# A two-layer diffusion trunk on one core: the first layer's gates and ups by seven half-block products instead of eight

## The chip, the core and the metric

The kernel runs on one core of a Trainium2 chip. The core has five engines with instruction streams of their own: TensorE (PE, matrix products; PEld is its weight load), VectorE (DVE), ScalarE (ACT), GpSimd (POOL) and SyncE (SP), which here issues all DMA transfers between DRAM and on-chip memory. Matrix products collect in PSUM, everything else stands in SBUF. The metric is the device time of one execution in microseconds. The kernel before takes 2279.43 us (median of 3 runs, 2278.52 to 2282.81).

## The reference

A trunk of two layers over 512 latent and 256 context tokens of width 1024, all in 32-bit floats. Each layer has an adaptive norm, one input projection for three mixers (RWKV-7, latent attention, mLSTM), one output projection, a second adaptive norm and a SwiGLU feed-forward network of hidden width 2816. What matters here is the second half of a layer:

```python
xl = xl + gt1_l * (concatenate([ya_l, yb_l, ym_l]) @ w_out[i])
xl = xl + gt2_l * swiglu(modulate(rmsnorm(xl, norm2_g[i]), sh2_l, sc2_l), ffn_w_in[i], ffn_w_out[i])
if ctx_out:                      # layer 0 alone: the context tokens too, with their own modulation
    ...
def swiglu(h, w_in, w_out):
    gate, up = jnp.split(h @ w_in, 2, axis=-1)
    return (jax.nn.silu(gate) * up) @ w_out
```

The modulation's vectors (`sh`, `sc`, `gt`, six of width 1024 for each layer) are products of `silu(c)` and `silu(c_ctx)` with a 1024 x 6144 matrix per layer. So layer 0's feed-forward network works on 768 tokens, layer 1's on 512.

## The kernel before

Everything is kept transposed: 128 features on the partitions, tokens along the free dimension. A 32-bit product is made of three products in a rounded format: each operand is split into `hi` (a rounded copy, by ScalarE) and `lo` (the rest, by VectorE; helper `split`, L227 and L228), and `gemm` (L262) adds hi·hi, hi·lo and lo·hi of each 128-row block of K in PSUM. `weight` (L235) loads a block of weights through a ring of two buffers and splits it.

The part that the change touches is the end of each layer, in one scope of the layer loop:

- **Output projection** (`add` with which = 0). `silu_rows` first spreads `silu(c)` over the partitions (transposes L311, copies L312), for the modulation's products on VectorE. Then for each of eight 128-row blocks m of the output: load and split the weights, 24 x 512 and 24 x 256 columns of matmul, residual sum on VectorE (L1323), squares and sums for the next norm (L337, L338; on POOL for the first four m). The last four m are worked span by span (first the 512 latent tokens, then the 256 context tokens), so that the norm of the first span is finished while the second is computed. `norm_page` multiplies X by the scale (L364, into one of three `hu` buffers), modulates it (L365) and splits it into the pages `hpage` (even pages on VectorE, odd ones on POOL).
- **Feed-forward network in three parts** of 8, 7 and 7 hidden tiles (PARTS). For a hidden tile j the gate's and the up's weights are loaded and split, and for each token span 24 + 24 matmuls run. tanh (L1490), two VectorE operations (L1491, L1492) and a split give the hidden tile as `hid`, of which eight stay in SBUF. After each part `add` with which = 1 multiplies the part's hidden tiles with the output weights for all eight m and adds them to X.
- **Modulation.** `mod_dve` loads 128 x 1024 weights (L318) and makes two VectorE products with row sums (L320), one for context and one for latent tokens. They fill VectorE's free time: four products (two blocks) after each hidden tile of layer 0, two after each m of the first two output parts, and what is left of them in the third.

All loops are written out at build time. A scheduler simulates the engines and sets the order of instructions on each of them; `issue_after` holds an instruction back until a given one was placed. SP's queue of DMA issues is in order too. PSUM has five buffers for these products (`gm`).

## Time and profile before

| What | us |
| --- | --- |
| Median of the runs (3) | 2279.43 |
| Profiled execution, its own time | 2283.55 |
| Its span, first to last instruction | 2281.8 |
| TensorE busy | 2159.2 (95%) |
| VectorE busy | 1381.9 (61%) |
| ScalarE busy | 844.7 (37%) |
| GpSimd busy | 314.2 (14%) |

Outside the span lie 1.75 us of the profiled execution. It was 4.1 us longer than the median of the runs, so a difference worked out in the trace is taken from 2283.55 and then brought to the median. Busy time alone does not say what a stage is worth. The stage of the change is layer 0's feed-forward network, from 747 to 1307 us of the span, and the rows further down are mostly read from there.

### The profile page before, as it was taken

The numbers are of one execution on the slowest core, as the hardware profiler recorded it, in microseconds if no ns is written. First come the engines' busy times: TensorE is split into PE (matmuls) and PEld (weight loads), VectorE is DVE, ScalarE is ACT, GpSimd is POOL, SyncE is SP. The second block draws the span as 40 slices with busy tenths as digits, with TensorE's granted clock in tenths as the row PEclk, the third lists the DMA queues.
The fourth block names the chain that finished last, engine by engine and source line by source line (L and its number), as shares of the span: only waits on it lengthen the run. The fifth ranks groups of instructions, "written<-read, shape, count | busy, mean of one in ns | idle before, by whom it ended". The sixth has DMA issues, their size and how long they took to land.

```text
span 2281.8 us, 36365 instructions
## 1 busy us (share of the span) xinstructions
PE 2159.2 (95%) x14604; PEld 1780.9 (78%) x14604; DVE 1381.9 (61%) x2706; ACT 844.7 (37%) x1527; POOL 314.2 (14%) x482
## 2 busy tenths in 40 slices
PE   7999997997999999999999999999898998999999
PEld 4788886784668788888888878787685677888887
DVE  6687777895547766554444455788796545334343
ACT  4433333664552421122122354433473544222231
POOL 1022322332201100000000111113142211000000
PEclk9999997897999999999999989999697998999999
DMA  7241112232115334344432312211232122323323
GB/s 289 84 153 52 62 41 74 77 88 56 42 70 155 100 114 146 111 129 135 133 112 83 109 52 63 73 57 39 85 100 59 35 74 83 101 94 94 100 92 102
DMA packets 87352, 211.99 MB, mean 93 GB/s; under 512 B 10248, under 2 KB 33680, under 8 KB 86544
## 3 DMA queue, kind: packets, MB, share of 16 engines
q1 hardware_dynamic: 87184, 209.67, 29.2%
q8 instruction: 115, 1.88, 0.3%
q14 instruction: 53, 0.43, 0.1%
HBM read 187.62 MB, written 22.02 MB: 92 GB/s over the span
## 4 chain that ended last, share of the span: by engine, by line
PE 81%; DVE 10%; ACT 4%; DMA 2%; issue 2%; POOL 1%; SPq 0%; DVEq 0%; ACTq 0%; POOLq 0%
PE gm L262 57%; PE po L1034 4%; PE psm L585 2%; PE inv L660 2%; PE st L1028 1%; DVE cT L320 1%; PE st L1029 1%; PE st L1030 1%; PE mx L1008 1%; PE psm L514 1%; PE pB L700 1%; DVE wl L228 1%; PE psm L573 1%; ACT hu L365 1%; PE up L246 1%
## 5 line engine op out<-in xcount | busy, mean ns | idle before, releaser
L262 PE MATMUL gm<-hpage,wh 128*128 128x512 f32 (+1 forms) x3744 | 1001.7, 355 | 15.3 <-ACT hpage L227 8.9
L262 PEld LDWEIGHTS gm<-hpage,wh 128*128 128x128 f32 x3744 | 664.2, 191 | 119.8 <-ACT hpage L227 11.0
L262 PE MATMUL gm<-hpage,wl 128*128 128x512 f32 (+1 forms) x1872 | 657.4, 353 | 1.9 <-DVE wl L228 1.8
L227 ACT ACTIVATE wh<-wr 128x1024 fp32r<-128x1024 f32 (+2 forms) x214 | 221.6, 1036 | 560.7 <-PE gm L262 457.6
L262 PEld LDWEIGHTS gm<-hpage,wl 128*128 128x128 f32 x1872 | 358.1, 191 | 50.6 <-DVE wl L228 2.5
L228 DVE TENSOR_TENSOR wl<-wr,wh 128x1024 fp32r<-128x1024 f32 (+2 forms) x214 | 258.2, 1207 | 186.9 <-ACT wh L227 185.1
L262 PE MATMUL gm<-hid,wh 128*128 128x512 f32 (+1 forms) x1056 | 282.6, 356 | 0.0
L262 PEld LDWEIGHTS gm<-hid,wh 128*128 128x128 f32 x1056 | 185.6, 188 | 32.2
L262 PE MATMUL gm<-hid,wl 128*128 128x512 f32 (+1 forms) x528 | 187.4, 356 | 0.0
L1323 DVE SCALAR_TENSOR_TENSOR X<-gm,mod,X 128x512 f32<-128x512 f32 (+1 forms) x100 | 64.0, 643 | 191.0 <-PE gm L262 187.7
L320 DVE CUSTOM_DVE_ANT_0 cT<-wd,cB,mod_b 128x1024 f32<-128x1024 f32 x140 | 177.7, 1300 | 1.1 <-DMA wd<-in_mod_d 0.7
L1492 DVE SCALAR_TENSOR_TENSOR ft<-ft,gm 128x512 f32<-128x512 f32 x66 | 39.5, 598 | 153.0 <-PE gm L262 152.7
L1010 DVE TENSOR_REDUCE mr<-mx 128x1 fp32r<-128x768 f32 (+1 forms) x80 | 67.9, 848 | 83.8 <-PE mx L1008 83.6
L1034 PE MATMUL po<-pe,hpage 128*128 128x512 f32 (+1 forms) x224 | 112.2, 590 | 0.5 <-ACT pe L1032 0.4
L262 PEld LDWEIGHTS gm<-hid,wl 128*128 128x128 f32 x528 | 99.0, 188 | 16.1
L338 POOL TENSOR_TENSOR acc<-acc,sq 128x512 f32<-128x512 f32 (+1 forms) x15 | 23.9, 1601 | 604.0 <-ACT sq L337 604.0
L1032 ACT ACTIVATE pe<-st 128x512 f32<-128x512 f32 (+1 forms) x112 | 62.9, 563 | 89.8 <-PE st L1030 88.7
L227 ACT ACTIVATE hid<-ft 128x512 fp32r<-128x512 f32 x66 | 36.2, 549 | 128.4 <-DVE ft L1492 128.4
L1028 PE MATMUL st<-k,k 97*128 97x512 f32 (+1 forms) x112 | 78.0, 698 | 4.7 <-ACT k L1015 4.1
L1490 ACT ACTIVATE ft<-gm 128x512 f32<-128x512 f32 x66 | 33.9, 514 | 90.4 <-PE gm L262 90.3
L1008 PE MATMUL mx<-k,k 96*128 96x256 f32 (+1 forms) x144 | 46.3, 396 | 17.1 <-DVE mr L1010 9.9
L585 PE MATMUL psm<-pr,kb 64*128 64x128 f32 (+1 forms) x384 | 57.7, 308 | 1.4 <-POOL pr L555 1.4
(425 smaller groups left out, 3128.5 us busy)
## 6 DMA issues: line engine op xcount, KB each, us to landing
wr<-in_ffn_in SPq DMA_DIRECT2D x88, 512.0 KB, 3.5
wd<-in_mod_d SPq DMA_DIRECT2D x86, 512.0 KB, 3.8
wr<-in_w_in SPq DMA_DIRECT2D x44, 512.0 KB, 3.6
wr<-in_ffn_out SPq DMA_DIRECT2D x34, 448.0 KB, 3.4
wr<-in_w_out SPq DMA_DIRECT2D x20, 512.0 KB, 3.7
wr<-in_ffn_out SPq DMA_DIRECT2D x16, 512.0 KB, 3.6
zs<-ze SPq DMA_DIRECT2D x26, 256.0 KB, 2.0
X<-in_xT SPq DMA_DIRECT2D x16, 384.0 KB, 6.4
```

The costliest lines, as they stand in the source:

```text
L227: ac.activation(hi, src, AF.Copy)
L228: return en.tensor_tensor(lo, src, hi.bitcast(F32), ALU.subtract)
L262: pe.matmul(ps, x[:, j], act[k][y][:, a:b], start=(i == 0 and n == 0), stop=(i == len(kl) - 1 and n == 2))
L320: ve.tensor_tensor_reduce(out=t[:, s], in0=w, in1=cb[:, s], scale=1.0, scalar=modb[:, l, m:m + 1], op0=ALU.mult, op1=ALU.add, accum_out=mo ...
L585: pe.matmul(pa[j][:, p, c], flat(kb[hr, d, p, c]), flat(pr[hr, d, p, c, 0:nq]), start=True, stop=True)
L660: i = pe.matmul(v8(o)[hr, q], a[hr, d, p, c], b[hr, d, p, c], start=True, stop=True)
L1008: pe.matmul(ps[:, a - k0:b - k0], qh[0:96, n * P:(n + 1) * P], kh[0:96, a:b], start=True, stop=True)
L1010: ve.tensor_reduce(mr[:, n - q0:n - q0 + 1], ps[:, :T - k0], AX.X, ALU.max)
L1028: pe.matmul(ps, kh[0:97, ks], qh[0:97, qs], start=True, stop=False)
L1032: ac.activation(e, ps, AF.Exp, scale=QK_SCALE)
L1034: pe.matmul(po[:, :w], v, e, start=(kt == kts[0]), stop=(kt == kts[-1]))
L1323: return ve.scalar_tensor_tensor(X[:, m, a:b], ps, mods[l][:, 24 * which + 16 + m, s:s + 1], X[:, m, a:b], ALU.mult, ALU.add)
```

## The change

In layer 0 the second half is written anew (`ffn`, with `residuals`, `halves`, `resplit`, `gate_up`, `swiglu`, `fetch` and `mods_on`); layer 1 keeps the old loops. Two hidden tiles are computed as before (PLAIN = 2). For the other 20, the gate's and the up's weights of one tile are read as one matrix of 2 x 2 blocks (gate and up by two halves of K, 128 x 512 each), the normed tokens as another (two halves of K by two halves of 384 tokens), and Winograd's form of Strassen's product is used: seven products of half blocks in place of eight, with sums of blocks before and after.

- The token sums are made once (`halves`): eight subtractions on VectorE, eight on POOL, and twelve splits on VectorE and ScalarE. For this the normed pages are kept unsplit in `ru`.
- The weight sums are made for each tile: four on POOL, of 128 x 512. Five half blocks of weights are split beside the gate's whole block.
- Each product is 4 K blocks x 3 matmuls of 384 columns. Out of PSUM come one copy on ScalarE and seven sums on VectorE; then two tanh, two VectorE operations of 384 columns and one of 768.
- The hidden tiles go unsplit to DRAM (`hd`), and come back split in the output parts (`fetch`, `resplit`). X goes to DRAM after the output projection (`xm`) and comes back ahead of the output parts. All 22 hidden tiles are now computed before the first output part.
- The modulation's products leave the hidden tiles of layer 0. They stand in the output projection (as before), in the three output parts (two blocks to an m), and the last 16 blocks in layer 1's output projection and its first eight hidden tiles. `silu_rows` is run twice in layer 0's second half (ahead of the output projection and ahead of the first output part) and once in layer 1's, where before it was run once, in layer 0's.

```diff
-                hl = split(hh[:, 0, a:b], hh[:, 1, a:b], t2)
-                mod_some(2, tmp, 3, hl)
+    def halves(l, nt, ru, h, tq):
+        n = nt // 2
+        for k in range(4):
+            b11, b12, b21, b22 = ru[:, k, :n], ru[:, k, n:nt], ru[:, k + 4, :n], ru[:, k + 4, n:nt]
...
+            ve.tensor_tensor(b11, b12, b11, ALU.subtract)
+            gp.tensor_tensor(t3, b22, b12, ALU.subtract)
+            ve.tensor_tensor(b22, b22, b11, ALU.subtract)
+            gp.tensor_tensor(b21, b21, b22, ALU.subtract)
+            for t, src in ((t1, b11), (t2, b22), (t4, b21)):
+                split(t[:, 0], t[:, 1], src)
...
+            h = add(0, w_out, yh, KORD, lambda m: None, lambda m, i: mod_some(2, i), (l, 1), ru, last)
+            for k in range(KD):
+                sp.dma_start(out=xm[:, k, :nt], in_=X[:, k, :nt])
+            w0 = gate_up(l, 0, last)
+            with behind(last):
+                ts = halves(l, nt, ru, h, tq)
...
+                gh, gl, g = weight(I["ffn_in"][l, j, 0], KD, P, raw=True)
+                sp.dma_start(out=u, in_=I["ffn_in"][l, j, 1])
+                gp.tensor_tensor(s1, u[:, 0:4], u[:, 4:8], ALU.add)
+                gp.tensor_tensor(s2, s1, g[:, 0:4], ALU.subtract)
+                gp.tensor_tensor(s3, g[:, 0:4], u[:, 0:4], ALU.subtract)
+                gp.tensor_tensor(s4, g[:, 4:8], s2, ALU.subtract)
+                A = {1: (gh[:, 0:4], gl[:, 0:4]), 2: (gh[:, 4:8], gl[:, 4:8])}
+                for i, src in ((6, s2), (7, s3), (5, s1), (4, u[:, 4:8]), (3, s4)):
+                    t = ws.tile([P, 2, 4, P], F32R, name="ws", bufs=7)
+                    split(t[:, 0], t[:, 1], src)
...
+                    for k in range(4):
+                        for x, y in ((0, 0), (0, 1), (1, 0)):
+                            pe.matmul(ps, A[i][x][:, k], B[i][k][y], start=(k == 0 and x + y == 0),
+                                      stop=(k == 3 and x == 1))
...
+                ac.activation(c1, product(1), AF.Copy)
+                ve.tensor_tensor(c2, c1, product(6), ALU.add)
+                ve.tensor_tensor(c1, c1, product(2), ALU.add)
+                ac.activation(t1, c1, AF.Tanh, scale=0.5)
+                ve.scalar_tensor_tensor(t1, t1, 1.0, c1, ALU.add, ALU.mult)
+                ve.tensor_tensor(c3, c2, product(7), ALU.add)
+                p5 = product(5)
+                ve.tensor_tensor(ups[:, n:nt], c3, p5, ALU.add)
+                ve.tensor_tensor(c2, c2, p5, ALU.add)
+                ve.tensor_tensor(ups[:, 0:n], c3, product(4), ALU.add)
+                ve.tensor_tensor(g2, c2, product(3), ALU.add)
+                ac.activation(t2, g2, AF.Tanh, scale=0.5)
+                ve.scalar_tensor_tensor(t2, t2, 1.0, g2, ALU.add, ALU.mult)
+                ve.scalar_tensor_tensor(hid[:, :nt], hid[:, :nt], 0.5, ups[:, :nt], ALU.mult, ALU.mult)
+            sp.dma_start(out=hd[j, :, :nt], in_=hid[:, :nt])
+        first = [fetch(l, j, nt, hq, "hq") for j in range(4)]
...
+        for k in range(KD):
+            sp.dma_start(out=X[:, k, :nt], in_=xm[:, k, :nt])
+        mods_on(st.enter_context(pool(f"md{l}1", 1, "right")), pm)
...
+            def before(m):
+                if part == 0:
+                    mod_some(1)
+            def done(m, ins):
+                more(1)
+                mod_some((1, 2, 2)[part], ins)
...
+    def fetch(l, j, nt, pool, name):
+        t = pool.tile([P, 2, T], F32R, name=name)
+        sp.dma_start(out=t[:, 1, :nt].bitcast(F32), in_=hd[j, :, :nt])
+        resplit(t[:, :, :nt])
```

What moves in the engines' order stands in the next pieces. Line numbers in those of the kernel after are its own: `split` is L228 and L229 there, the norm's product L367, the products' sums L1535 to L1547.

VectorE at the second norm, in the kernel before: the norm's products (L364, three `hu` buffers) and the remainders of pages (L228 `hpage`).

```order
L1323 SCALAR_TENSOR_TENSOR X<-gm,mod_85,X 128x256
L364 TENSOR_TENSOR hu<-X,psm 128x512 x3
L228 TENSOR_TENSOR wl<-wr,wh 128x1024
L338 TENSOR_TENSOR acc<-acc,sq 128x256
L228 TENSOR_TENSOR hpage<-hu,hpage 128x512
L364 TENSOR_TENSOR hu<-X,psm 128x512
L228 TENSOR_TENSOR hpage<-hu,hpage 128x512
```

The same place in the kernel after, where the products (L367) fill `ru`.

```order
L1328 SCALAR_TENSOR_TENSOR X<-gm,mod_85,X 128x256
L367 TENSOR_TENSOR ru<-X,psm 128x512 x8
L341 TENSOR_TENSOR acc<-acc,sq 128x256
L229 TENSOR_TENSOR wl<-wr,wh 128x1024
L229 TENSOR_TENSOR hpage<-ru,hpage 128x512 x2
L352 TENSOR_SCALAR ms<-ss 128x2
```

All eight products of the latent span now stand ahead of the first page's remainder, where there were three.

VectorE in the steady run of hidden tiles, in the kernel before: the gate's and the up's operations, two weight remainders (`wl`), the remainders of `hid`, and the modulation (L320; the row of 128x1 reads out the sum).

```order
L1491 SCALAR_TENSOR_TENSOR ft<-ft,gm 128x512
L1492 SCALAR_TENSOR_TENSOR ft<-ft,gm 128x512
L228 TENSOR_TENSOR hid<-ft,hid 128x512
L228 TENSOR_TENSOR wl<-wr,wh 128x1024
L1491 SCALAR_TENSOR_TENSOR ft<-ft,gm 128x256
L1492 SCALAR_TENSOR_TENSOR ft<-ft,gm 128x256
L228 TENSOR_TENSOR wl<-wr,wh 128x1024
L228 TENSOR_TENSOR hid<-ft,hid 128x256
L320 ISA cT_7078,mod_85<-wd,cB,mod_b 128x1024
L320 ISA mod_85 128x1
L320 ISA cT_7078,mod_85<-wd,cB,mod_b 128x1024
L320 ISA mod_85 128x1
```

The same in the kernel after, one tile from its first sum out of PSUM (L1535) almost to the last.

```order
L1535 TENSOR_TENSOR c_10720<-c_10719,gm 128x384
L229 TENSOR_TENSOR ws<-wsum,ws 128x512
L1536 TENSOR_TENSOR c_10719<-c_10719,gm 128x384
L229 TENSOR_TENSOR wl<-wr,wh 128x1024
L1538 SCALAR_TENSOR_TENSOR hid<-hid,c_10719 128x384
L1539 TENSOR_TENSOR c_10721<-c_10720,gm 128x384
L229 TENSOR_TENSOR ws<-wu,ws 128x512
L1541 TENSOR_TENSOR ups<-c_10721,gm 128x384
L1542 TENSOR_TENSOR c_10720<-c_10720,gm 128x384
L229 TENSOR_TENSOR ws<-wsum,ws 128x512
L1543 TENSOR_TENSOR ups<-c_10721,gm 128x384
L1544 TENSOR_TENSOR c_10722<-c_10720,gm 128x384
```

The modulation is gone from here, and between the sums out of PSUM stand the remainders of one whole and five half weight blocks, of a later tile.

SP's queue at the passage from hidden tiles to the output part, in the kernel before: weights (`wr`, L235) and the modulation's weights (`wd`, L318).

```order
L235 DMA wr<-in_ffn_in 128x1024 x2
L318 DMA wd<-in_mod_d 128x1024 x2
L235 DMA wr<-in_ffn_in 128x1024 x2
L318 DMA wd<-in_mod_d 128x1024 x2
L235 DMA wr<-in_ffn_out 128x1024 x2
L318 DMA wd<-in_mod_d 128x1024 x2
L235 DMA wr<-in_ffn_out 128x1024 x2
```

The same in the kernel after, where L1592 fetches hidden tiles back, L1548 stores them and L1556 reads X back.

```order
L1592 DMA hpage<-hd 128x768 x4
L236 DMA wr<-in_ffn_out 128x1024
L1592 DMA hq_11395<-hd 128x768
L1592 DMA hq_11465<-hd 128x768
L1592 DMA hpage<-hd 128x768 x3
L321 DMA wd<-in_mod_d 128x1024 x3
L1592 DMA hpage<-hd 128x768
L1592 DMA hq_11535<-hd 128x768
L1548 DMA hd<-hid 128x768
L321 DMA wd<-in_mod_d 128x1024
L236 DMA wr<-in_ffn_out 128x1024
L1556 DMA X<-xm 128x768 x8
```

Eleven fetches of hidden tiles, a store and four of the modulation's blocks now stand in the queue, with two output weights, ahead of X's eight blocks.

## Rows read from the trace of the kernel before

**Rows 1.** The page: span, busy times, chain that ended last

```profile
span 2281.8 us, 36365 instructions
PE 2159.2 (95%) x14604; PEld 1780.9 (78%) x14604; DVE 1381.9 (61%) x2706; ACT 844.7 (37%) x1527; POOL 314.2 (14%) x482
...
PE 81%; DVE 10%; ACT 4%; DMA 2%; issue 2%; POOL 1%; SPq 0%; DVEq 0%; ACTq 0%; POOLq 0%
```

**Rows 2.** Windows of 50 us: busy (instructions) by engine, granted clock, DMA share, GB/s

```profile
core 0: us, PE busy (x) PEld busy (x) DVE busy (x) ACT busy (x) POOL busy (x), PEclk, DMA share, GB/s
0.00:50.00 50.00, 34.49 (x158) 18.92 (x158) 34.44 (x77) 21.00 (x38) 3.67 (x8) 1.00 0.86 330
750.00:800.00 50.00, 48.39 (x252) 41.03 (x252) 33.40 (x62) 20.83 (x38) 7.01 (x7) 0.96 0.28 87
1000.00:1050.00 50.00, 50.00 (x290) 44.25 (x289) 24.27 (x37) 11.78 (x18) 0.00 (x0) 1.00 0.41 127
1300.00:1350.00 50.00, 44.15 (x232) 36.39 (x231) 30.26 (x66) 30.55 (x54) 9.74 (x23) 0.86 0.23 69
```

**Rows 3.** Timeline, ScalarE: gate tanh of two successive tiles (start, us, instruction)

```profile
1027.41 0.60 ACT L1490 ACTIVATE ft<-gm 128x512 f32<-128x512 f32 x1 [4.28 <-PE gm L262]
...
1044.09 0.60 ACT L1490 ACTIVATE ft<-gm 128x512 f32<-128x512 f32 x1 [4.28 <-PE gm L262]
```

**Rows 4.** Timeline, TensorE: the lo products of successive K blocks, 512 and 256 columns

```profile
715.65 0.40 PE L262 MATMUL gm<-hpage,wl 128*128 128x512 f32 x1
...
716.34 0.40 PE L262 MATMUL gm<-hpage,wl 128*128 128x512 f32 x1
...
740.99 0.28 PE L262 MATMUL gm<-hpage,wl 128*128 128x256 f32 x1
...
741.35 0.28 PE L262 MATMUL gm<-hpage,wl 128*128 128x256 f32 x1
```

**Rows 5.** Groups by line and shape, 760 to 1300 us (busy, mean ns | idle, releaser)

```profile
L320 DVE CUSTOM_DVE_ANT_0 cT<-wd,cB,mod_b 128x1024 f32<-128x1024 f32 x80 | 100.0, 1279 | 0.4
...
L228 DVE TENSOR_TENSOR wl<-wr,wh 128x1024 fp32r<-128x1024 f32 x50 | 61.2, 1224 | 37.2 <-ACT wh L227 37.2
...
L1323 DVE SCALAR_TENSOR_TENSOR X<-gm,mod,X 128x512 f32<-128x512 f32 x24 | 18.0, 750 | 49.3 <-PE gm L262 49.3
...
L228 DVE TENSOR_TENSOR hid<-ft,hid 128x512 fp32r<-128x512 f32 x22 | 15.2, 692 | 14.7 <-ACT hid L227 14.7
...
L1492 DVE SCALAR_TENSOR_TENSOR ft<-ft,gm 128x512 f32<-128x512 f32 x22 | 15.1, 688 | 88.7 <-PE gm L262 88.6
...
L1323 DVE SCALAR_TENSOR_TENSOR X<-gm,mod,X 128x256 f32<-128x256 f32 x21 | 10.2, 484 | 34.8 <-PE gm L262 34.8
...
L1492 DVE SCALAR_TENSOR_TENSOR ft<-ft,gm 128x256 f32<-128x256 f32 x22 | 9.3, 421 | 6.8 <-PE gm L262 6.8
```

**Rows 6.** Timeline of POOL, DVE and PE in the output projection, then POOL after it

```profile
710.10 3.61 POOL L338 TENSOR_TENSOR acc<-acc,sq 128x512 f32<-128x512 f32 x2 [4.95 <-ACT sq L337]
...
710.83 2.30 DVE L320 CUSTOM_DVE_ANT_0 cT<-wd,cB,mod_b 128x1024 f32<-128x1024 f32 x1
...
713.06 1.73 DVE L228 TENSOR_TENSOR wl<-wr,wh 128x1024 fp32r<-128x1024 f32 x1
...
714.85 0.50 PE L262 MATMUL gm<-hpage,wl 128*128 128x512 f32 x1 [1.75 <-DVE wl L228]
...
748.42 1.27 POOL L228 TENSOR_TENSOR hpage<-hu,hpage 128x512 fp32r<-128x512 f32 x1 [34.71 <-ACT hpage L227]
```

**Rows 7.** Timeline at the second norm and at the second hidden tile

```profile
744.36 1.88 DVE L364 TENSOR_TENSOR hu<-X,psm 128x512 f32<-128x512 f32 x3 [0.41 <-PE psm L356]
...
747.18 0.93 PE L262 MATMUL gm<-hpage,wh 128*128 128x512 f32 x2 [2.85 <-ACT hpage L227]
...
747.63 0.68 DVE L228 TENSOR_TENSOR hpage<-hu,hpage 128x512 fp32r<-128x512 f32 x1
...
770.16 0.73 PE L262 MATMUL gm<-hpage,wh 128*128 128x512 f32 x2 [0.80 <-ACT wh L227]
```

**Rows 8.** Timeline: the silu rows' transposes and copies before the output projection

```profile
668.59 1.09 PE L311 MATMUL psm<-c_id,sc 128*128 128x128 f32 x8
...
671.13 1.08 ACT L312 ACTIVATE cB<-psm 128x512 f32<-128x512 f32 x2
```

**Rows 9.** DMA issues of the page: line, count, KB each, us to landing

```profile
wr<-in_ffn_in SPq DMA_DIRECT2D x88, 512.0 KB, 3.5
...
X<-in_xT SPq DMA_DIRECT2D x16, 384.0 KB, 6.4
```

More of the change, by code (lines that the diff above doesn't have):

```diff
@@ L1342, in behind, with residuals, add @@
         return st
+    def residuals(l, nt, X, tmp, pm, pgm):
+        def add(which, get, act, order, before, each, after=None, raw=None, ends=None):
+            if after is not None:
+                rng = spans(nt) if nt > TL else ((0, 256), (256, 512))
+                acc = tmp.tile([P, T], F32, name="acc", bufs=1)
+                last = KD - 4
+            else:
+                last = KD
+            for m in range(last):
+                before(m)
+                for ps, a, b in gemm(pgm, get(m), act, spans(nt), order):
+                    i = residual(l, which, X, m, ps, a, b)
+                    if after is not None:
+                        norm_stat(acc, X, m, a, b, tmp, gp)
+                each(m, i)
+            if after is None:
+                return
+            gain(*after)
+            hn, tail = None, [(m, None) for m in range(last, KD)]
+            for a, b in rng:
+                held = []
+                for m, w in tail:
+                    w = w or get(m)
+                    held.insert(0, (m, w if m >= KD - 2 else None))
+                    for ps, _, _ in gemm(pgm, w, act, ((a, b),), order):
+                        residual(l, which, X, m, ps, a, b)
+                        norm_stat(acc, X, m, a, b, tmp, ve)
+                tail = held
+                if hn is None:
+                    hn = pages(KD)
+                bc = norm_scale(acc, ((a, b),), pm)[0][0][0]
+                for k in range(KD):
+                    i = norm_page(*after, X, hn, bc, k, a, b, tmp, raw)
+                    if ends is not None:
+                        ends[k % 2:k % 2 + 1] = [i]
+            return hn
+        return add
@@ L1378, in trunk, with mod_some @@
     marks = (md, mm)
+    moving.update(p=xm0, cb=(cb, t), bufs=4)
     todo = [(0, m) for m in range(16, 48)] + [(1, m) for m in range(48)]
[L1381 to L1383 removed]
+    def mod_some(n, ins=None):
+        with behind([ins] if ins is not None else ()):
             for _ in range(min(n, len(todo))):
[L1385 removed]
+                mod_dve(*todo.pop(0), *moving["cb"], moving["p"], moving["bufs"])
     for l in range(DEPTH):
```

233 lines of the change are left out of this document (140 added, 93 removed).

## The prediction

> **What bounds the kernel now.** I read the page's busy times and chain first, then windows over layer 0's feed-forward network, then its timeline row by row. The page gives TensorE 95% of the span and 81% of the chain that ended last [rows 1]. The windows say where that is strict: from 1000 to 1050 us TensorE is busy for all 50 us at full granted clock, beside VectorE 24.27, ScalarE 11.78 and POOL 0 [rows 2]. So in the run of hidden tiles only matmul columns cost time, and the other engines have room. Two tanh of the same shape lie 1044.09 - 1027.41 = 16.68 us apart [rows 3]: one tile, 96 matmuls, 48 of 512 and 48 of 256 columns, 36,864 columns, 0.4525 ns each. At the norm ahead of it the picture is another: in 750 to 800 the clock is 0.96 and VectorE has 33 us.
>
> **The tiles.** A tile now has 7 x 4 x 3 = 84 matmuls of 384 columns, 32,256. Is 384 as cheap per column as the mix of before? Three matmuls take 0.69 us at 512 columns and 0.36 at 256 [rows 4], 0.449 and 0.469 ns a column; 384 lies between, so 0.4525 may stand. 32,256 x 0.4525 ns = 14.60 us. The gain is 2.08 us a tile, and 20 x 2.085 = -41.7 us. At the two ends, 0.449 and 0.469, a tile takes 14.5 or 15.1 us (-44 to -31).
>
> This holds if TensorE stays the bound. VectorE's tile: seven sums out of PSUM and two gated operations of 384 columns at 0.555 (mean of 0.688 and 0.421 for 512 and 256 [rows 5]), one operation of 768 at 0.96 (the same line drawn on), one weight remainder at 1.22, five half ones at 0.69: 5.00 + 0.96 + 1.22 + 3.46 = 10.6 us. The modulation (four products of 1.28 a tile) is gone from here. POOL has four sums of 128 x 512; alone it took 1.27 for such an operation [rows 6], so 5.1 us.
>
> The two disturb each other. In the output projection two POOL sums (512 and 256 wide, by columns 1.9 us alone) took 3.61; meanwhile VectorE's 1.28 us product took 2.30 and the 1.22 us remainder 1.73, and TensorE then waited 1.75 us for that remainder [rows 6]. VectorE lost 1.02 + 0.51 = 1.53 us to some 2 us of POOL's work, 0.77 for each. Of VectorE's 10.6 us, 6.8 have two inputs in SBUF (remainders, gated operations); the seven sums have one in PSUM. If only those 6.8 are stopped, the loss is 5.1 x 0.77 x 0.64 = 2.5 us, and VectorE has 13.1 of 14.6 us. That is close (90%), but TensorE has five PSUM buffers and weights more than half a tile ahead, so I take 14.60. Bounds: no loss, and the full 5.1 us, 15.7 a tile.
>
> The Trainium skill, page "SBUF — State Buffer", section "Who interferes with whom", speaks against the change here: a VectorE instruction with two SBUF inputs contends with a GpSimd instruction that reads SBUF, and the shared port pair is an exclusive lock; with at most one SBUF input it does not contend. The rows on the 2.30 and 1.73 us operations agree with the first half; none tests the second. By the rule taken at its worst, each POOL sum would stop VectorE whole, which is the 15.7 us above and the second case below.
>
> ScalarE has 11.78 of 50 us now [rows 2], about 4 in a tile; even doubled it is not near. Weights are still 1 MB a tile, a hidden tile stored adds 0.39: 1.44 MB in 14.6 us is 99 GB/s, and the kernel's first 50 us moved 330 [rows 2]. Nothing.
>
> **The start.** Before the change three norm products stood ahead of the first page's remainder (1.88 us); now eight do. The five more cost 5 x 0.63 = 3.1 us, and the remainder, which was at 747.63 [rows 7], comes some 3.4 us later, with the small sum and the weight remainder between. TensorE starts its second matmul with that page; nothing covers it. Behind that, VectorE makes eight subtractions and twelve remainders of 384 columns (20 x 0.555 = 11.1 us), with POOL's eight subtractions beside them. Half of these stand ahead of the weight remainders of tile 1, where TensorE already waits 0.80 us for a weight now (at 770.16, [rows 7]). I count +3.5: the first remainder late, the halves hidden behind tiles 0 and 1 (33 us). Bounds: 0, if pages that then come without a pause give it back, and +10, if five of the subtractions' and remainders' microseconds fall on tile 1 as well and POOL adds 1.5.
>
> **Silu rows.** One run has 16 transposes and four copies. Eight transposes took 1.09 us, two copies 1.08 [rows 8]. Two more runs: 2.2 us each on TensorE. The one ahead of the output parts goes partly into the last tiles and I take +1.6; the one in layer 1 +2.2. Layer 1's output projection also gets eight modulation products (1.28 each, two for an m); TensorE has 5.6 us there for an m (24 x 512 columns), VectorE about 2 x 1.28 + 1.22 + 0.75 + POOL's disturbance of about 1 = 5.5: +0.7 (0 to +4).
>
> **The passage to the output parts.** TensorE's last tile reads the pages until near its end, and the hidden tiles can come back into them only after product 7, the fourth of seven: 3 x 2.085 = 6.2 us ahead of the end. X's first block stands in SP's queue behind eleven fetches and a store (0.39 MB each), four modulation blocks and two output weights (0.52 each); with itself 8.26 MB. At 330 GB/s that is 25 us, so X arrives 19 us after the first output part begins; at 250, 27 us. Until then no residual sum frees PSUM. TensorE has five buffers: two m with two spans each and one span more, 2.67 x 8.34 (half of 16.68, as half the columns) = 22 us. So at 330 it does not stop for PSUM. Behind the sum waiting on VectorE stand weight remainders; the fourth m needs its own at 25 us, and VectorE, once X is there, needs 4 x 1.28 + 1.22 + 0.75 + 0.48 = 7.6 us for an m [rows 5] against TensorE's 8.34, with splits of fetched tiles (0.96 each) besides. It catches up slowly. I take +3; bounds 0 (X in time) and +10 (250 GB/s, 27 - 22 = 5, and as much again in late weights). X's own row, eight blocks of 384 KB issued together with a median of 6.4 us to landing [rows 9], says that such bursts run near the high end.
>
> **Sum.** -41.7 + 3.5 + 1.6 + 2.2 + 0.7 + 3 = -30.7. The profiled execution took 2283.55 (span 2281.8 [rows 1]), so 2252.9; it was 4.1 above the median of the runs, so 2249. The likeliest case's own range is 2240 to 2262.
>
> **The rivals.**
> - *VectorE becomes the bound* through POOL's sums. For it: 90% on one in-order engine, and a remainder that TensorE already waited for. Against: TensorE's waits in those rows came with a full modulation load besides. At 15.0 to 15.7 us a tile the gain shrinks by 8 to 22 us: 2257 to 2271, middle 2264. Chance 0.17. The Trainium skill's rule named above ("SBUF — State Buffer", "Who interferes with whom") is the mechanism that would do it.
> - *The passage is late.* X at 200 GB/s, 35 us after the start: TensorE stops 13 us instead of 3, and its clock falls after such a stop; the window at 1300 to 1350, with a norm's stops, has 0.86 [rows 2]. 2259 to 2264. Chance 0.08.
> - *Slower.* POOL stops VectorE also in the sums out of PSUM, and each POOL sum takes 1.8 us (half of the pair's 3.61 [rows 6]), during which VectorE stands: 10.6 + 4 x 1.8 = 17.8 us a tile, 1.1 more than now; 20 x 1.1 + 11 (start, silu rows and passage as above) = +33, 2312. It decides from 16.7 - 11/20 = 16.1 us a tile on. Against it: both engines made headway in the 3.61 us. Chance 0.05.
> - *No net change*: tiles at 15.5 (-24), the start and the passage at their upper bounds and the silu rows as above (+24.5). Chance 0.05.
>
> **How the numbers follow.** Likeliest 0.65: 2249. What a measurement of this kernel can tell from no change is about 0.2%, 4.6 us. Faster by more than that are the likeliest, the first rival and the second: 0.65 + 0.17 + 0.07 = 0.89. The same 0.05, slower 0.06. The range reaches up to the first rival's end, 2272, and down to 2238, which is tiles at 14.5 (-2), a start without loss (-3.5), and a passage without loss (-3), less some; it holds the likeliest and the first two rivals, all but a tenth of their chance, about 0.82.
>
> **What the profile after would show.** Right: windows in the middle of the hidden tiles with TensorE busy 50 of 50 at full clock, the 768-column operation every 14.6 us, VectorE at 35 to 45 of 50. A TensorE idle time released by VectorE's `ws` or by a PSUM sum in each tile would show the first rival; the duration of sums out of PSUM beside POOL decides the third (0.55 or more than 1). At the second norm: an idle time of TensorE of about 6.3 us (2.85 before [rows 7]) released by the page's remainder. At the passage: TensorE idle for VectorE's sum into X or for weights, at most some 5 us in all, and X landing about 19 us in. The prediction is wrong if a tile takes over 15 us, or if layer 1, whose work hardly changes, differs by more than 5 us.

## The result and the profile after

The changed kernel takes 2254.15 us (median of 4 runs, 2251.05 to 2255.75), the kernel before 2278.97 beside it; the ratio is 0.9888, with a 95% interval of 0.987 to 0.9907. Timed again later (j below), it was 0.9875 (0.9858 to 0.9891), 2257.08 against 2286.60 us. So it is 1.1 to 1.3% faster: 24.8 us in the first timing and 29.5 in the second, where 30.4 were forecast.

The profiled execution took 2254.63 us, 28.9 less than the profiled one of before. Where these 28.9 us lie can be read from TensorE's instructions at the stages' borders (the norm's transposes, L356 before and L359 after, the first matmuls of a tile, the first with a hidden tile):

| Stage | Before | After | Difference |
| --- | --- | --- | --- |
| Start to the second norm of layer 0 | 743.3 | 744.6 | +1.4 |
| Norm to tile 1's first matmul | 26.9 | 30.3 | +3.4 |
| Tile 1 and the stop behind it | 17.5 | 22.6 | +5.1 |
| Tiles 2 to 21 (before at the steady 16.68) | 333.6 | 296.1 | -37.5 |
| Output parts to the next layer's norm | 185.8 | 186.6 | +0.7 |
| Layer 1: mixers | 547.2 | 541.3 | -5.9 |
| Layer 1: output projection to the norm | 46.1 | 47.9 | +1.8 |
| Layer 1: norm to the first output part | 101.8 | 104.0 | +2.2 |
| Layer 1: first output part to the last product | 275.4 | 275.4 | 0 |

The page of the kernel after has these lines, which answer to [rows 1]:

```profile
span 2252.8 us, 36651 instructions
PE 2112.4 (94%) x14396; PEld 1776.7 (79%) x14396; DVE 1539.0 (68%) x2908; ACT 901.6 (40%) x1629; POOL 444.7 (20%) x570
...
PE 77%; DVE 13%; ACT 3%; issue 3%; DMA 2%; POOL 1%; SPq 0%; DVEq 0%; ACTq 0%; POOLq 0%
```

TensorE has 46.8 us less work and VectorE 157 more; the share of the chain that is TensorE's fell from 81% to 77%, and VectorE's rose to 13%. The windows of the kernel after (columns as in [rows 2]) show the start and the steady run:

```profile
750.00:800.00 50.00, 40.99 (x214) 35.50 (x215) 38.39 (x63) 26.63 (x54) 23.98 (x19) 0.88 0.21 69
800.00:850.00 50.00, 49.63 (x279) 49.31 (x278) 47.63 (x58) 20.57 (x35) 23.73 (x16) 0.98 0.41 132
950.00:1000.00 50.00, 50.00 (x288) 50.00 (x287) 37.99 (x55) 19.22 (x31) 21.48 (x15) 1.00 0.33 106
```

In the steady run TensorE is busy 50 of 50 us at full clock, as before, with VectorE at 37.99 and POOL at 21.48. From 800 to 850 VectorE is full (47.63), and from 750 to 800 TensorE lacks 9 us, against 1.6 before. TensorE's own rows show two of the places. In order of time: the norm's stop, its two aftermaths in the first tile, and the stop ahead of tile 2:

```profile
748.62 0.73 PE L265 MATMUL gm<-hpage,wh 128*128 128x512 f32 x2 [2.94 <-ACT hpage L228]
751.57 0.99 PE L349 MATMUL ss<-c_sel,acc 128*128 128x1 f32 x4 [2.22 <-DVE acc L341]
753.22 0.80 PE L265 MATMUL gm<-hpage,wh 128*128 128x512 f32 x1 [0.66 <-DVE hpage L229]
...
797.51 1.01 PE L1527 MATMUL gm<-hpage,wh 128*128 128x384 f32 x2 [4.74 <-ACT wh L228]
798.32 2.12 PE L1527 MATMUL gm<-t,ws 128*128 128x384 f32 x6
```

The first stop is that of before (2.85 in [rows 7]); then TensorE waits 2.22 us for a VectorE sum that stands behind the eight products, and 0.66 for the page's remainder. At 797.51 it waits 4.74 us for ScalarE's `hi` of the gate weight. The six matmuls behind it take 2.12 us, half the rate of the steady run; short windows show the granted clock there at 0.50, the lower of TensorE's two levels (1.2 and 2.4 GHz):

```profile
799.50:801.50 2.00, 2.00 (x7) 2.00 (x7) 2.00 (x5) 2.00 (x5) 0.79 (x1) 0.50 0.00 0
801.50:803.50 2.00, 2.00 (x11) 2.00 (x11) 2.00 (x3) 1.02 (x2) 1.37 (x2) 0.86 0.84 238
```

Back to the `hi` that TensorE waited for. It had its weight already: it stands on ScalarE behind the `hi` of a weight sum. The chain of waits from 780 to 800 us, cut to its large pieces, says what that one waited for (start, us, what):

```profile
785.59 1.96 DVE t L229 x4
...
787.57 5.54 DMA wu<-in_ffn_in
...
793.25 1.27 POOL wsum L1513
...
794.59 1.27 POOL wsum L1514
...
795.88 0.64 ACT ws L228
```

The last seven remainders of the halves end at 787.55; only then is the first up weight issued, its data need 5.5 us, and two POOL sums follow. What SP waited for in this stretch stands in its waits (line waited for: us, times, longest):

```profile
SPq L1592 <- DMA hd<-hid: 2.2, 1, 2.2
SPq L1548 <- DVE hid L1423: 1.7, 1, 1.7
SPq L1511 <- DVE t L229: 1.1, 1, 1.1
```

SP was held by tile 0's store (L1548), by the fetch of the same tile back (L1592), and by a remainder of the halves (L1511 <- DVE t). The load of the up weights uses no result of the halves, so it can only wait for its buffer, which lies in memory that `ru` held. In the tiles, the groups by line (columns as in [rows 5], 900 to 1050 us) have the two operations that share with POOL and one of the sums out of PSUM:

```profile
L229 DVE TENSOR_TENSOR ws<-wsum,ws 128x512 fp32r<-128x512 f32 x42 | 29.8, 710 | 4.0 <-ACT ws L228 3.6
...
L1547 DVE SCALAR_TENSOR_TENSOR hid<-hid,ups 128x768 f32<-128x768 f32 x10 | 19.3, 1928 | 0.3
L1513 POOL TENSOR_TENSOR wsum<-wu 128x512 f32<-128x512 f32 x10 | 18.9, 1895 | 0.8
...
L1515 POOL TENSOR_TENSOR wsum<-wr,wu 128x512 f32<-128x512 f32 x11 | 14.2, 1291 | 56.1 <-DVE ws L229 56.1
...
L1536 DVE TENSOR_TENSOR c<-c,gm 128x384 f32<-128x384 f32 x10 | 5.5, 554 | 7.0 <-PE gm L1527 7.0
```

The 768-column operation with two operands in SBUF takes 1.93 us, where the same line drawn on from [rows 5] gave 0.96; the POOL sum beside it (L1513) 1.90, another that meets hardly more than sums out of PSUM (L1515) 1.29. The sums out of PSUM stay at 0.55.

### The profile page after: what moved, and what is told of

It is laid out like the page before. It is cut to its first block, busy times and chain, and to the rows that moved or that the text cites. A ratio compares the mean times of both kernels' runs of the same rounds, so it can differ in the third digit from the quotient of the medians.

```text
span 2252.8 us, 36651 instructions
## 1 busy us (share of the span) xinstructions
PE 2112.4 (94%) x14396; PEld 1776.7 (79%) x14396; DVE 1539.0 (68%) x2908; ACT 901.6 (40%) x1629; POOL 444.7 (20%) x570
## 4 chain that ended last, share of the span: by engine, by line
PE 77%; DVE 13%; ACT 3%; issue 3%; DMA 2%; POOL 1%; SPq 0%; DVEq 0%; ACTq 0%; POOLq 0%
PE gm L265 42%; PE gm L1527 11%; PE po L1039 4%; PE psm L590 2%; PE inv L665 2%; DVE cT L323 1%; PE st L1033 1%; DVE wl L229 1%; PE st L1034 1%; PE st L1035 1%; PE mx L1013 1%; PE psm L519 1%; PE pB L705 1%; PE up L249 1%; PE up L250 1%
## 5 line engine op out<-in xcount | busy, mean ns | idle before, releaser
L265 PE MATMUL gm<-hpage,wh 128*128 128x512 f32 (+1 forms) x2816 | 774.1, 360 | 18.6 <-ACT hpage L228 12.0
L265 PEld LDWEIGHTS gm<-hpage,wh 128*128 128x128 f32 x2816 | 501.9, 191 | 103.9 <-ACT hpage L228 14.1
L265 PE MATMUL gm<-hpage,wl 128*128 128x512 f32 (+1 forms) x1408 | 503.1, 358 | 2.7 <-DVE wl L229 2.6
L228 ACT ACTIVATE wh<-wr 128x1024 fp32r<-128x1024 f32 (+2 forms) x194 | 200.3, 1033 | 526.2 <-PE gm L265 398.3
L229 DVE TENSOR_TENSOR wl<-wr,wh 128x1024 fp32r<-128x1024 f32 (+2 forms) x194 | 244.0, 1258 | 141.7 <-ACT wh L228 132.2
L265 PEld LDWEIGHTS gm<-hpage,wl 128*128 128x128 f32 x1408 | 269.2, 191 | 44.2 <-DVE wl L229 4.2
L1527 PE MATMUL gm<-t,ws 128*128 128x384 f32 x720 | 133.2, 337 | 0.0
L1527 PEld LDWEIGHTS gm<-t,ws 128*128 128x128 f32 x720 | 127.3, 190 | 0.0
L265 PE MATMUL gm<-hid,wh 128*128 128x512 f32 x352 | 110.6, 395 | 0.0
L228 ACT ACTIVATE ws<-wsum 128x512 fp32r<-128x512 f32 x80 | 49.8, 630 | 107.3 <-PE gm L1527 81.9
L1527 PE MATMUL gm<-hpage,ws 128*128 128x384 f32 x480 | 91.3, 339 | 0.0
L265 PE MATMUL gm<-hq,wh 128*128 128x512 f32 (+1 forms) x352 | 87.2, 338 | 0.0
L265 PEld LDWEIGHTS gm<-hid,wh 128*128 128x128 f32 x352 | 66.0, 187 | 16.1
L229 DVE TENSOR_TENSOR ws<-wsum,ws 128x512 fp32r<-128x512 f32 x80 | 66.9, 837 | 9.4 <-ACT ws L228 8.9
```

Source lines behind the costliest of these rows:

```text
L228: ac.activation(hi, src, AF.Copy)
L229: return en.tensor_tensor(lo, src, hi.bitcast(F32), ALU.subtract)
L265: pe.matmul(ps, x[:, j], act[k][y][:, a:b], start=(i == 0 and n == 0), stop=(i == len(kl) - 1 and n == 2))
L1527: pe.matmul(ps, A[i][x][:, k], B[i][k][y], start=(k == 0 and x + y == 0), stop=(k == 3 and x == 1))
```

## The experiments

Short names below are letters. "Network" is the time of layer 0 from its second norm to the next layer's first, 563.9 us before, 535.5 after; it is the measure for edits at the start, because the whole kernel's time also carries layer 1's granted clock (further down). "Stop" is the time from the start of the last matmul ahead of tile 2 to the start of the first one of it: 5.0 us in after, of which the row above counts 4.74 as idle. Nine of the runs are single executions; i, j and l have four or five.

### Are the seven products worth what was forecast, and who bounds a tile?

**d: all 22 tiles plain, the rest of the change kept.**

```diff
-PLAIN = 2
+PLAIN = 22
-            with behind(last):
-                ts = halves(l, nt, ru, h, tq)
```

> All 22 tiles as the first two (96 matmuls), no halves made; everything else of the change stays: hidden tiles through DRAM, all tiles ahead of the first output part, X stored and read back, the modulation spread anew, ru kept. This is the change without its seven products. If the seven products are worth 20 x 2.02 = 40.4 us in the tiles and cost 9 to 12 us around tiles 2 to 5, this kernel takes 2254 + 40 - 10 = 2284, with tiles of 16.68 us. Rival: the moved modulation alone changes the time (layer 1's output projection with its norm +3.3 us, layer 1's mixers -5.9 us in the trace after): if the mixers' 5.9 us belong to the change, they show here too; if they come of the granted clock of that one execution (0.75 before, 0.86 after in the same 866 matmuls), they may not.

Measured: 2290.89 us. The 2284 expected belong to a before of 2279; here the kernel before took 2286.09 beside it. The network takes 566.9 us, 3.0 more than before, and 31.4 more than after. Tile 1 begins 30.05 us after the norm, as in after (30.3; before 26.9). So the norm's part of the start (+3.2) is there without any halves; the seven products bring 40.4 us in the tiles and lose 9 of it again, 8.1 around tiles 1 to 5 and 0.9 in the output parts. The mixers of layer 1 take 546.5 us here, as before.

**h: the half blocks' remainders twice.**

```diff
                     split(t[:, 0], t[:, 1], src)
+                    ve.tensor_tensor(t[:, 1], src, t[:, 0].bitcast(F32), ALU.subtract)
```

> The five remainders of half weight blocks are computed twice in each of the 20 tiles (the second overwrites the first with the same numbers): VectorE gets 5 x 0.69 = 3.5 us more a tile, so 10.9 to 11.3 measured busy plus 3.5 = 14.4 to 14.8, plus what POOL takes of the added ones. This asks how much room VectorE had: if the tile is TensorE's, and VectorE's room is the 3.6 us that its busy time shows, the tile grows only a little, to 14.7 to 15.5 us (kernel 2255 to 2272). If POOL's sums stop VectorE for their whole length (5.1 us a tile), VectorE needs 10.6 + 3.5 + 5.1 = 19 us and the tile goes there (kernel 2340).

Measured: 2288.35 us; from tile 12 on a tile takes 16.25 us. Both numbers given were missed. A window of this kernel (columns as in [rows 2]):

```profile
950.00:1000.00 50.00, 47.73 (x260) 44.69 (x261) 49.65 (x66) 15.29 (x27) 19.18 (x12) 1.00 0.27 88
```

VectorE is busy 49.65 of 50 us and TensorE no longer is. So VectorE is the bound here, and 16.25 - 3.46 = 12.8 us a tile are left for the rest of its work. The forecast had 13.1. The 12.8 are an upper figure, because POOL held up two of the added remainders too (1.67 and 1.66 us instead of 0.69). The busy time in after shows only 11.1 (37.99 x 14.66 / 50): there POOL's sums hold up one long operation a tile, by 1 us, and two more by 0.05, and here four, by 0.6 to 1.0 us each.

**g: the weight sums on VectorE.**

```diff
-                gp.tensor_tensor(s1, u[:, 0:4], u[:, 4:8], ALU.add)
+                ve.tensor_tensor(s1, u[:, 0:4], u[:, 4:8], ALU.add)
```

and the same for the other three sums.

> The four weight sums of a tile on VectorE instead of POOL. VectorE then has 10.6 + 4 x 0.69 = 13.4 us a tile and POOL nothing. If the shared use with POOL is what stretches the 768-column operation from 0.96 to 1.93 us, it falls to 0.96 here, and VectorE is busy 13.4 of 14.66 (45.7 of 50 us) with the tile still at 14.66. Rival (VectorE is nearer its limit than its busy time says, in-order waits between sums and remainders): the tile grows to 15 to 15.5 us, the kernel by 7 to 17 us. In tiles 2 to 5, where VectorE was full (48 of 50 us), it should lose 2 to 4 us in either case. Kernel 2255 to 2258 by the first, 2262 to 2272 by the second.

Measured: 2254.19 us, tiles 14.66, network 533.5. The 768-column operation, with POOL at rest, and the window:

```profile
L1547 DVE SCALAR_TENSOR_TENSOR hid<-hid,ups 128x768 f32<-128x768 f32 x10 | 9.5, 952 | 0.0
```

```profile
950.00:1000.00 50.00, 50.00 (x288) 50.00 (x287) 42.80 (x69) 19.43 (x31) 0.00 (x0) 1.00 0.34 104
```

0.95 us instead of 1.93: the use shared with POOL made the difference. VectorE has 42.8 of 50 us, 12.5 a tile, and TensorE still bounds. The four sums are 2.76 us of that, so VectorE's own work undisturbed is 9.8 us; in h, 9.8 + 3.5 = 13.3 became 16.25, so as an estimate from g and h, 5.1 us of POOL's work cost a full VectorE about 3 us, 0.6 for each (the forecast had 0.77 for each, and 2.5 in all by the share of operations that it can hit). Against the expectation, the start did not lose by it: tile 2 came 2.0 us earlier than in after.

### What holds TensorE ahead of tile 2?

**a: the pool of the weight sums on the other side of memory; b: SP's queue; c: both.**

```diff
-        ws = st2.enter_context(pool(f"ws{l}", 2))
         fp = st2.enter_context(pool(f"f{l}", 1, "right"))
+        ws = st2.enter_context(pool(f"ws{l}", 2, "right"))
```

```diff
+                if j == PLAIN:
+                    with behind([d]):           # d: the up weights' DMA
+                        for i, x in enumerate(early_hid):
+                            sp.dma_start(out=hd[i, :, :nt], in_=x[:, :nt])
...
-        first = [fetch(l, j, nt, hq, "hq") for j in range(4)]
+        with behind([held]):                    # held: the up weights' DMA of tile 8
+            first = [fetch(l, j, nt, hq, "hq") for j in range(4)]
```

> The only edit: the pool with the weight sums and the up's raw weights lies over the freed modulation buffers, not over ru. In the changed kernel the first up weight of tile 2 is issued at 787.57 us, as the last remainder of the halves has read ru, and TensorE stands 5.02 us ahead of tile 2; tile 2 then takes 16.87 us instead of 14.66. Theory B (the buffer over ru alone): the issue comes right after the one ahead of it in SP's queue, near 782, and the 5.02 us shrink to about 1. Theory Q (SP's queue in order: the store of tile 0 and its fetch stand ahead, and the fetch goes at 786.16): the issue moves by only 1.4 us, the stop to 3.6. Steady tile 14.66 in both; whole kernel 2248 by B, 2253 by Q.

> The only edit: the stores of tiles 0 and 1 stand behind the up weights of tile 2 in SP's queue, and the four early fetches of hidden tiles behind those of tile 8. Theory B (buffer over ru): nothing changes, the issue waits for ru until 787.6 and the stop stays 5.0 us. Theory Q (SP's queue): the issue moves up to 782 and the stop shrinks to about 1 us. Both together, theory BQ: 5.0 here, 3.6 with the buffer moved alone, and about 0 to 1 only where both are gone. Whole kernel 2254 (B, BQ) or 2248 (Q).

> Both edits: pool moved off ru, and SP's queue freed of stores and fetches ahead of tile 2's up weights. Theory BQ: the up weights are issued at about 781 to 783, behind the gate weight's buffer, POOL's sums start near 786, the stop ahead of tile 2 falls from 5.0 to under 1 us, TensorE keeps its full clock, and tile 2 takes 14.7 to 15.5 us: 6 to 7 us less, 2247. Rival H (the halves' work on VectorE, POOL and ScalarE is itself too late, whatever the weights): the stop stays over 3 us, released by a remainder or a hi of the halves or of ws.

Measured: a 2254.41 (network 536.4, stop 5.2 us), b 2252.78 (531.6, 3.2 us), c 2261.04 (534.0, 3.1 us). In a and c the first up weight was still issued 42.6 us after the norm, and SP's waits in c name the halves' remainders once more:

```profile
SPq L1516 <- DVE hid L1423: 9.4, 1, 9.4
SPq L1512 <- DVE t L229: 5.7, 1, 5.7
```

So the edit of a had not done what it was meant to: by SP's wait, the first buffers still lay over `ru` in a pool on that side. Nothing can be said from a on theory B. In b the issue hardly moved, as theory B has it: 42.4 us after the norm, 42.9 in after. What went is transfer time, 1.8 us of it (5.54 us in after, chain above):

```profile
783.93 3.72 DMA wu<-in_ffn_in
```

Whether the queue's order did that is not shown. In f and k, further down, SP's queue is the same at this place, with the store and the fetch ahead of the up weights, and the transfer takes 3.63 us in f and 5.28 in k. So theory Q is out for the issue, and open for the transfer.

**e: as c, the up weights in a pool of their own, which lies over the modulation's old buffers.**

```diff
+        wup = st2.enter_context(pool(f"wu{l}", 1, "right"))
...
-                u = ws.tile([P, KD, P], F32, name="wu", bufs=2)
+                u = wup.tile([P, KD, P], F32, name="wu", bufs=2)
```

> As 'c_place_and_order', but with the up weights in a pool of their own that lies over the freed modulation buffers, since in the two runs before it they still waited for the last remainder of the halves (issue 41.8 us after the norm began, in after, a and c alike). Theory B (that buffer is what holds the first up weights back): the issue now comes 36 to 37 us after the norm (behind the gate weight's buffer, which comes free there), POOL's sums end near 44, the stop of TensorE ahead of tile 2 falls from 5.0 (3.1 in b and c) to 0 to 1 us, and tile 2 runs at full clock: 14.7 to 15.2 us. Tiles from the norm to the first output part: 341 to 342 us against 348.2 in after and 344.2 in b. Rival H (halves too late): stop over 2.5 us, released by a remainder of the halves or of the norm's pages.

Measured: 2249.79 us; network 531.3; stop 1.7 us, tile 2 15.6 us. The up weights are no longer late. What is left of the stop stands in POOL's waits:

```profile
POOL wsum L1521 <- DVE t L229: 3.3, 1, 3.3
```

POOL's first sum waits 3.3 us for a remainder of the halves. It reads the up weights alone, so again only its result buffer can lie over `ru`. The theory holds, one buffer further on. Of the steps expected, the issue went further forward than thought (ahead of the first tile's weights, so that these came later: the norm's stop was 4.45 us here, 2.94 in after).

### The norm, layer 1's modulation, and a version that has it all

**f: the norm's products in the old order, and no modulation in layer 1. k: the first edit of f alone.**

```diff
-                    i = norm_page(*after, X, hn, bc, k, a, b, tmp, raw)
+                    with behind(lows[k - 3:k - 2] if raw is not None and k >= 3 else ()):
+                        i = norm_page(*after, X, hn, bc, k, a, b, tmp, raw)
+                    lows.append(i)
...
-                mod_some((1, 2, 2)[part], ins)
+                mod_some((1, 2 if m < 4 else 4, 4)[part], ins)
```

> Two edits far apart, read by stage. (1) Norm: the norm's product of page k stands behind the remainder of page k - 3, as the three hu buffers enforced before the change. If the eight products in a row are what delays the first remainder, the 2.6 us stop of TensorE in the first tile (748.96 to 751.57 in after) goes and the two plain tiles end about 3 us earlier; if not (rival: the halves behind them delay tile 1 by as much), the stops only move to tile 1. (2) Modulation: the 16 blocks left for layer 1 go into layer 0's output parts (4 to an m in the second half of part 1 and in part 2), and layer 1 has neither silu rows nor modulation. If modulation and silu rows cost layer 1's output projection, its 47.9 us go back to 46.1 and the stage behind it from 104.0 to 101.8; if the spread itself (another order there) does, they stay. The output parts of layer 0 take 186.5 us if VectorE has the room, up to 190 if not.

> The norm's order alone (first edit of f, modulation as in the change). Layer 1's output projection should take 47.8 again and the stage behind it 104, as in after, where f without modulation there had 46.3 and 102.3; the output parts of layer 0 188.3 instead of f's 196.8; the tiles from the norm to their end 340.9 as in f. Sum against after: -6.3 at the start, 2248 if layer 1's mixers take 541 us, 2254 if 547.

Measured: f 2266.82, k 2262.84. The norm's order does what was thought: tile 1 begins 26.1 and 26.2 us after the norm (30.3 in after, 26.9 before), and the network is 531.3 in k, 4.2 us less than in after where 6.3 were expected. The stop ahead of tile 2 is not the norm's: 4.5 us of it stay in k (1.3 in f, where the up weight's transfer is 1.65 us shorter and tile 2 begins that much earlier). Without modulation layer 1's output projection takes 46.3 (47.8 in k), but the output parts of layer 0, which took it over, 195.0 instead of 186.5: the spread of the change is the better one. What was not expected: layer 1's mixers take 554.2 and 553.0 us.

**i: all three edits at the start. j: the changed kernel again. l: i without the norm's edit.**

```diff
-                d = sp.dma_start(out=u, in_=I["ffn_in"][l, j, 1])
+                with behind(mark):              # mark: the DMA of tile 1's last weights
+                    d = sp.dma_start(out=u, in_=I["ffn_in"][l, j, 1])
```

> Three edits at the start of the hidden tiles together, modulation as in the change: the norm's product of page k behind the remainder of page k - 3 (as in f), the up weights of tiles 2 and on over the freed modulation buffers and, for tile 2, in SP's queue right behind tile 1's weights, stores and early fetches behind them (as in e). In e the stop ahead of tile 2 fell from 5.0 to 1.7 us and tile 2 from 21.2 (stop included) to 16.7; in f the norm part alone brought tile 2 2.0 us forward (44.8 us after the norm's scale instead of 46.8) and 20 tiles from the norm to their end 6.3 us. Both together: the first output part starts 338 to 341 us after the norm against 347.2 in after, and the kernel takes 2247 against 2254 measured beside it. Rival: what is gained at the start is the same wait seen twice (in f the halves were done earlier, so SP's queue no longer mattered): then no more than f's 340.9. Rival, slower: the two-level clock in layer 1 (mixers 541 or 547 us with the same instructions) covers it; then the medians differ by under 3 us.

> The changed kernel itself, unedited, timed beside the one before it in this list and the kernel before: 2251 to 2256 as measured. Its trace shows once more whether layer 1's mixers take 541 us (granted clock 0.86 in the stretch of 866 matmuls) or 547 (0.76): if both are seen with identical instructions, the 5.9 us by which the mixers were shorter in the trace after are the clock's and not the change's.

> The start mended without the norm's edit: up weights over the freed modulation buffers and behind tile 1's weights in SP's queue, stores and early fetches behind them. In i the norm's edit made the scheduler draw another order of layer 1's mixers (552.5 and 553.0 us in i and k, 541 to 548 in after, b, c and e), and that ate the 8.3 us gained in layer 0. Here TensorE's order is the change's own to the last instruction. If the order was the cause, layer 1's mixers take 540 to 548 us again, the network of layer 0 takes 529 to 531 against 535.5, and the kernel's ratio to before is 0.9845 to 0.9865 where the change has 0.9875 beside it. Rival (the clock alone: whoever gives TensorE fewer stops in layer 0 gets a lower granted clock in layer 1): the mixers take 550 us or more here too, with the order unchanged, and the ratio stays at 0.9875.

Measured:

| Kernel | Median us | Ratio to before (95%) | Network | Mixers of layer 1 |
| --- | --- | --- | --- | --- |
| after, first timing | 2254.15 | 0.9888 (0.987 to 0.9907) | 535.5 | 541.3 |
| j, the same again | 2257.08 | 0.9875 (0.9858 to 0.9891) | 535.5 | 539.5 |
| i | 2258.73 | 0.9878 (0.9862 to 0.9893) | 527.2 | 552.5 |
| l | 2252.12 | 0.986 (0.9833 to 0.9886) | 530.7 | 541.8 |

In i the stop ahead of tile 2 is gone, and 8.3 us of the network. Its mixers give 11 to 13 us back, the same as k's: the norm's edit changes what the scheduler simulates, and it wrote another order for layer 1's mixers, the same in i and k. With TensorE's order the change's own (l), the mixers take 541.8 and 4.8 us of the network stay. The mixers go with the order and not with the missing stops: k keeps the stop ahead of tile 2 and has i's order and i's mixers, and after with the eight runs that keep its order (a, b, c, e, g, h, j and l) has 539.5 to 547.9. How the other order costs its time is open; the granted clock in the stretch shown further down is 0.74 in i and k. l has the best median, but its interval overlaps that of the change; at this spread of runs 4 us is not proved to reach the whole kernel's time.

## Why the prediction was right, and where it was off

**The tiles: right.** 14.60 us a tile were forecast, 14.66 measured, 84 matmuls of 384 columns at 0.4545 ns a column. -41.7 against -40.4 us. TensorE stayed the bound, with VectorE near enough that 3.5 us more of work tipped it (h). The first rival, which needed 15.0 us or more, did not come. (The chance of the late passage stands as 0.08 in its own line and as 0.07 in the sum, that of slower as 0.05 and 0.06; it changes nothing here.)

**The shared use with POOL: right in kind.** VectorE's operations with two operands in SBUF grew beside POOL's sums and those out of PSUM did not (0.55 us, as forecast), so the third rival is out. How they grew can be read from one meeting in the steady run of after:

```profile
963.17 0.55 DVE L1546 SCALAR_TENSOR_TENSOR hid<-hid,c 128x384 f32<-128x384 f32 x1
963.76 1.93 DVE L1547 SCALAR_TENSOR_TENSOR hid<-hid,ups 128x768 f32<-128x768 f32 x1
...
963.34 1.54 POOL L1516 TENSOR_TENSOR wsum<-wr,wsum 128x512 f32<-128x512 f32 x1 [2.71 <-DVE ws L229]
964.95 1.89 POOL L1513 TENSOR_TENSOR wsum<-wu 128x512 f32<-128x512 f32 x1
```

Each of the last three ends when its own length alone (0.95 for L1547, 1.26 to 1.29 for POOL's) is added to the end of the one that ran before it on the other engine, less 0.11 to 0.14 us. So one stands until the other is done, and they take turns; neither runs slowly beside the other. The Trainium skill, page "SBUF — State Buffer", section "Who interferes with whom", has both halves of the rule and the exclusive lock, and here the rows agree with all three. What the lock costs VectorE is the rest of a POOL sum that is already running, not the whole length of every sum: 1 us a tile in after, about 3 of 5.1 in h. That "both engines made headway in the 3.61 us", as the prediction reads [rows 6], fits such turns too: VectorE's 2.30 and 1.73 us hold its own 1.28 and 1.22 behind one POOL sum each.

**The start: the step that was mis-sized.** +3.5 was forecast, with "the halves hidden behind tiles 0 and 1", and 0 to +10 as bounds. The first remainder came 3.5 us late (VectorE's first page, 7.9 us after the norm began against 4.4), where 3.4 were worked out, and tile 1 began 3.4 us late; TensorE's stops there are 2.94 + 2.22 + 0.66 = 5.8 us, where 6.3 were forecast. But the halves were not hidden: +5.1 us ahead of tile 2 and +2.9 in tiles 2 and 5 came on top (tile 2 took 16.87 us, its first 4 us at half clock after the stop, and tile 5 15.32, with a wait of 0.4 us for a sum of a full VectorE). In all 11.4 us (52.9 - 44.4, and 2.9), beyond the upper bound. I had looked for the lateness at tile 1's weights, where VectorE's order stood. It came one tile on, through memory: the new buffers of the weight sums are the old ones of the token sums, and so the first load and sum wait for the last remainder (chain and waits above; shown by e, in which the load is free of it and the stop shrinks to 1.7 us, and by i, in which the remainder that POOL's first sum then waits for also comes earlier, so that this sum begins 39.1 instead of 42.7 us after the norm in l, and the stop goes). The transfer of the up weight, 5.5 us here and 3.6 to 6.0 in the runs where it waits for the halves, is a part of the stop that the forecast had nowhere; why it varies is open. Its count of twelve remainders was also four short: four more, of the sums that go into the pages, run in tile 2 (from 799.02 us); no stop of TensorE there is theirs.

**The passage and the silu rows: too dear.** +3 and +1.6 were forecast, +0.7 measured in the output parts; eight of that silu run's sixteen transposes stand in tile 0 already (766.35 us). TensorE had no idle time in the output parts:

```profile
1100.00:1150.00 50.00, 50.00 (x288) 43.81 (x287) 45.10 (x70) 9.04 (x11) 0.00 (x0) 1.00 0.80 267
1150.00:1200.00 50.00, 50.00 (x293) 44.01 (x292) 47.83 (x74) 12.10 (x14) 0.00 (x0) 1.00 0.71 237
```

VectorE is busy 45 and 48 of 50 us, DMA at 0.80 and 0.71 of its share, and TensorE at 50. X came when it was reckoned to come:

```profile
1093.58 0.62 PE L265 MATMUL gm<-hq,wh 128*128 128x512 f32 x2
...
1105.89 5.49 SPq L1556 DMA_DIRECT2D X<-xm  x8
...
1112.12 1.14 DVE L1328 SCALAR_TENSOR_TENSOR X<-gm,mod,X 128x512 f32<-128x512 f32 x2 [4.90 <-issue]
```

The output part begins at 1093.58, X is issued 12.3 us later, and its first sum runs 18.5 us after the beginning, where 19 were reckoned. The five PSUM buffers, good for 22 us by the forecast, covered it; the +3 for what VectorE then has to catch up was not needed.

**Layer 1:** +2.9 forecast; +4.0 in the rows (1.8 and 2.2), and about 1.5 more that the table hides in the mixers' row. The silu rows' transposes stand there, ahead of the first output product: from the mixers' four matmuls of 1x1 to that product TensorE took 1.08 us before and 2.62 after. So 5.5 us in all. The output projection's part goes with the modulation and the silu rows (46.3 in f, 47.8 in k, which has them); the stage behind it does not (102.3 and 102.6), and moves with the order that the scheduler wrote (101.5 in d, 104.0 in after). That layer 1 as a whole came out 2 us shorter, inside the 5 us that the prediction allows, is the mixers' doing.

Put together: -40.4 + 11.4 + 0.7 + 5.5 = -22.8 us, where -30.7 were forecast. The medians differ by 24.8 and 29.5 us, the profiled executions by 28.9. The 6 us between the sum and the profiled pair are layer 1's mixers (-5.9 in the table, -7.4 without the transposes) and +1.4 at the beginning, which the change does not edit (740.1 to 749.4 us in the changed kernel and its variants). So that the whole time came so near the forecast is in part luck: the start and layer 1 cost 10.5 us more than forecast and the tiles gave 1.3 less, the passage and the silu rows gave back 3.9, and shorter mixers did the rest.

**Those 5.9 us are not shown to be the change's.** The same stretch of layer 1's mixers, 274 to 360 us behind the norm, in before, after and b (columns as in [rows 2]):

```profile
1581.00:1667.00 86.00, 72.86 (x862) 60.50 (x859) 67.64 (x176) 35.59 (x76) 18.99 (x36) 0.75 0.19 58
```

```profile
1554.00:1640.00 86.00, 66.91 (x894) 55.48 (x892) 71.57 (x190) 38.61 (x82) 22.40 (x40) 0.86 0.20 59
```

```profile
1547.00:1633.00 86.00, 70.72 (x875) 59.84 (x875) 68.14 (x179) 36.27 (x78) 18.63 (x36) 0.76 0.19 58
```

The granted clock is 0.75, 0.86 and 0.76; the mixers take 547.2, 541.3 and 546.4 us. After and b have the same order of TensorE's instructions throughout, and of VectorE's in all of layer 1. So the same work in the same order takes 5 us more or less here, and the granted clock goes with it; b has the change, and before's mixers. j, the same program as after, had 0.86 and 539.5 us once more, so two traces of one program with both clocks, which its expectation asked for, do not exist. The four executions of j lie between 2251.86 and 2260.20 us, with 0.964 for the span's clock in the shortest and 0.958 to 0.961 in the others. What grants the clock in one execution and not in another is open.

## What to carry to other kernels

Seven products for eight pay in full where TensorE is the strict bound and the other engines have the room for the sums; count that room in the engine's own work plus what a neighbour takes of it when it is full, not in its busy share. Where a change adds a preparation and then a steady run, ask for each first buffer of the run whose memory it was: a new pool over an old one hands the old one's last reader to the new one's first load. And compare stages, not only whole times: an edit in one place let the scheduler write another order over 500 us further on, which cost more than the edit gained.

## What the runs showed that was not expected

A stop costs more than its length: after 4.74 us without work tile 2 ran its first products at half the rate (six matmuls in 2.12 us, where 84 take 14.66), and took 16.87 us. In c the stop is 1.9 us shorter, and tile 2 still took 17.52. And a stage that no edit touches can differ by 5 us between kernels that run the same instructions in it in the same order, with the granted clock in it (0.86 or 0.76); that is more than most of the edits here were worth.
